# Three-neighbour interpolation on one core: fetching each batch's features 14 chunks ahead and casting them 3 chunks ahead, instead of both 6 chunks ahead

## The chip, the cores and the metric

The kernel runs on one core of one Trainium2 chip. The metric is device time in microseconds (us), lower is better. Three runs of the kernel before gave a median of 646.55 us (645.44 to 646.75).

## The reference

For each of 16 batches there are 1024 feature rows of 64 numbers, and 4096 queries. A query has three indices into the feature rows and three weights. Its result is the weighted sum of the three rows, with the weights divided by their sum:

```
weights_norm = weights / (weights_sum + 1e-8)
for b in range(batch):
    for i in range(n_query):
        for k in range(3):
            result[b, i] += weights_norm[b, i, k] * features[b, indices[b, i, k]]
```

Inputs and output are float32; the indices reach the kernel as 64-bit integers.

## The kernel before

The gather is done as a matrix product with a selection matrix that is made on the chip. The 4096 queries of a batch are cut into 8 chunks of 512, so there are 128 chunks, numbered i = 0 to 127; batch b begins at chunk a = 8b. Chunks are grouped by four (2048 queries, half a batch); only the first batch has smaller groups.

For a group, these steps follow one another:

- VectorE (DVE) prepares 16-bit codes from the indices and half-precision weights (prep, four batches at a time), and SyncE (SP) puts them into the scratch tensors code_d and wt_d.
- SP loads the codes of a group into the tile bcc (load_codes): one DMA of 1536 KB that broadcasts to all 128 partitions. It loads the weights into bcw (load_weights): two DMAs of 768 KB, one for each half of the partitions.
- ScalarE (ACT) turns codes into bytes y, one ACTIVATE for each chunk (stage1). DVE takes these apart into the four 8-bit selection matrices s (stage2).
- For each chunk, TensorE (PE) multiplies s by the batch's features f16 into the PSUM tile acc: 3 neighbours by 4 feature slices, 12 matmuls of 128x512 (main).
- acc is multiplied by the weights into x. For even chunks DVE reads acc directly; for odd chunks ACT first copies acc to xc (weight).
- Two chunks later PE sums the three neighbours and transposes with 12 small matmuls into pr. After every second chunk ACT copies pr to og, and SP writes og out (back).

The features of a batch come as one DMA of 256 KB into the tile fst (float32, two buffers), which ACT casts and halves into f16 (two buffers). In the kernel before, both are in load_features: the DMA and the cast are emitted at the same place.

The order of work on every engine is written out, and each engine works strictly in its order (InOrder, line 47). The list todo holds steps with a time in chunks. A step with time t is emitted in the iteration i that holds t: before the chunk's own work if its third entry is 0, and behind it if that entry is 1. Steps with negative times come before the chunk loop. Line 242 puts the codes at a - 12, line 243 the weights at a - 7, line 245 the features at a - 6 (a being the first chunk of the group, for line 245 of the batch), and line 247 stage1 of a group of four from a - 8 on, one chunk of it behind each iteration. For every batch but the first, the features step stands in iteration 8(b-1) + 2, the third iteration of the batch that is being worked on.

All loads and stores are issued by SP, also in order. A store of og waits on SP until ACT has written og, and whatever SP has to issue behind it waits as well. In the profile nearly every line is L55, the helper that records each operation, so operations are told apart by their tiles; f is f16, i_sb is the identity i2.

Of the kernel before, what the change touches and what calls it, by code (L numbers as in the profile page):

```python
# [9 lines left out]
P = 128  # L10
# [3 lines left out]
def kernel(  # L14
# [12 lines left out]
    fp32 = mybir.dt.float32  # L27
# [11 lines left out]
    J = 4  # L39
# [20 lines left out]
    sb = ctx.enter_context(tc.tile_pool(name="sb", bufs=2))  # L60
# [85 lines left out]
        for c in range(n // CH):  # L146
            owner[a + c] = (g, c)

    bcc, bcw, f16s, ys, ss = {}, {}, {}, {}, {}

    def load_codes(g):
        b, q, n, _ = groups[g]
# [12 lines left out]
                in_=wt_d.ap()[h, b, :, q:q + n].unsqueeze(0).to_broadcast([D, K, n]))  # L165

    def load_features(b):
        fst = sb.tile([P, J * P], fp32, bufs=2, name="fst")
        sp.dma_start(out=fst[:, :], in_=features[b].rearrange("(l x) d -> l (x d)", l=P))
        f16s[b] = sb.tile([P, J, P], fp16, bufs=2, name="f16")  # L170
        ac.mul(out=f16s[b].rearrange("p j m -> p (j m)"), in_=fst[:, :], mul=0.5)

# [64 lines left out]
    def at(time, engine, f, *args):  # L237
        todo.append((time, len(todo), engine, f, args))

    for g, (b, q, n, a) in enumerate(groups):  # L240
        m = n // CH
        at(a - 12, 0, load_codes, g)
        at(a - 7, 0, load_weights, g)
        if q == 0:
            at(a - 11.5 if b == 0 else a - 6, 0, load_features, b)
        for c in range(m):
            at(a - 2 * m + c if m == 4 else -8.5 + g / 10, 1, stage1, g, c)
        for j in range(J):
            at(a - m + (j * m // J | 1 if m == 4 else 0), 0, stage2, g, j)
# [78 lines left out]
```

## Time and profile before

| What | Value |
|---|---|
| Median of 3 runs | 646.55 us |
| Profiled execution | 649.85 us, of which its span (first to last instruction) is 647.9 us |
| Granted TensorE clock, mean | 0.837 of full speed |
| PE busy | 419.7 us, 65% of the span |
| ACT busy | 321.6 us, 50% |
| DVE busy | 306.5 us, 47% |
| DMA | 125.66 MB; the main queue's packets take 78.4% of the 16 engines' span |

Busy shares are means over the whole span. The features are cast 16 times, once a batch, so a batch's cycle can be read from one cast to the next. The chain of waits follows the work that ended last back to the start, and counts the time of each step on it. DMA share is the mean busy share of the 16 DMA engines; it can be somewhat over 1, since packets overlap.

### The profile page before, as it was taken

How to read it: one execution, taken by the hardware profiler on the slowest of the kernel's cores; microseconds unless marked ns; L12 is line 12 of the kernel's file. 1: busy time of each engine (PE TensorE's matmuls, PEld its weight loads, DVE VectorE, ACT ScalarE, POOL GpSimd, SP SyncE). 2: the span in 40 equal slices, each digit the busy share in tenths (PEclk: the TensorE clock that was granted, in tenths of full speed). 3: DMA queues.
4: the chain of work that ended last, by engine and by line, in shares of the span. 5: the costliest groups of instructions: out<-in, count | busy, mean ns of one | idle time of the engine just before them, and what ended most of it. 6: DMA issues, size and time to landing. Idle time of an engine off the chain costs nothing.

```text
span 647.9 us, 7370 instructions
## 1 busy us (share of the span) xinstructions
PE 419.7 (65%) x3072; PEld 211.8 (33%) x3072; DVE 306.5 (47%) x335; ACT 321.6 (50%) x274; POOL 0.2 (0%) x4
## 2 busy tenths in 40 slices
PE   0435492957859294793929649294875939387596
PEld 0112151523425152341514325152442515143253
DVE  4312380825537182662707338182643626164473
ACT  0531562818366370744718266371836547082642
POOL 0000000000000000000000000000000000000000
PEclk9967696997969698695968969798796959789698
DMA  5899495896959599695969959699795959669521
GB/s 89 221 207 251 134 267 113 227 251 167 267 150 283 135 240 218 151 263 132 272 138 201 278 117 279 129 230 228 188 270 137 265 133 260 166 178 267 128 62 66
DMA packets 70704, 125.66 MB, mean 194 GB/s; under 512 B 24080, under 2 KB 44048, under 8 KB 70672
## 3 DMA queue, kind: packets, MB, share of 16 engines
q1 hardware_dynamic: 70672, 125.20, 78.4%
q8 instruction: 24, 0.39, 0.3%
q14 instruction: 8, 0.07, 0.0%
HBM read 107.23 MB, written 17.96 MB: 193 GB/s over the span
## 4 chain that ended last, share of the span: by engine, by line
PE 41%; DMA 36%; ACT 10%; SPq 7%; issue 4%; DVE 2%; ACTq 0%
PE acc L55 37%; DMA fst<-in_features_dram 31%; SPq L55 7%; ACT y L55 4%; DMA bcc<-code_d 4%; PE pr L55 4%; ACT xc L55 4%; ACT og L55 1%; DVE x L55 1%; DVE s L55 1%; DMA code_d<-code 0%; DMA idx<-in_indices_dram 0%; ACTq L55 0%; ACT f L55 0%; DVE wn L55 0%
## 5 line engine op out<-in xcount | busy, mean ns | idle before, releaser
L55 PE MATMUL acc<-s,f 128*128 128x512 fp8e4 x1536 | 386.6, 406 | 222.8 <-ACT xc L55 196.7
L55 PEld LDWEIGHTS <-f 128*128 128x128 f16 x1536 | 151.0, 103 | 401.7 <-issue 244.7
L55 ACT ACTIVATE y<-bcc,lane_sb 128x1536 uint8<-128x1536 int16 x128 | 196.7, 1576 | 17.0 <-DMA bcc<-code_d 17.0
L55 DVE TENSOR_TENSOR x<-xc,bcw 128x1536 f16<-128x1536 f16 x64 | 61.3, 958 | 296.3 <-ACT xc L55 296.3
L55 ACT ACTIVATE f<-fst 128x512 f16<-128x512 f32 x16 | 10.1, 629 | 234.8 <-DMA fst<-in_features_dram 234.8
L55 ACT CAST xc<-acc 128x1536 f16<-128x1536 f32 x64 | 91.7, 1433 | 67.5 <-PE acc L55 67.5
L55 DVE TENSOR_SCALAR s<-y 128x1536 int32<-128x1536 int32 (+2 forms) x136 | 117.0, 904 | 15.4 <-ACT y L55 15.4
L55 DVE TENSOR_TENSOR x<-acc,bcw 128x1536 f16<-128x1536 f32 x64 | 112.2, 1753 | 20.8 <-PE acc L55 17.2
L55 PEld LDWEIGHTS <-x 128*128 128x128 f16 x1536 | 71.4, 117 | 30.6 <-DVE x L55 1.8
L55 PE MATMUL pr<-i_sb,x 128*128 128x64 f16 x1536 | 71.6, 197 | 1.7 <-DVE x L55 1.7
L55 ACT COPY og<-pr 128x512 f32<-128x512 f32 x64 | 37.8, 591 | 1.2 <-issue 1.2
L55 DVE RECIPROCAL wi<-ws 128x128 f32<-128x128 f32 (+2 forms) x5 | 3.9, 789 | 0.1
L55 DVE TENSOR_TENSOR wn<-wt,wi 128x128 f16<-128x128 f32 (+2 forms) x15 | 3.9, 284 | 0.1
L55 DVE COPY idk<-idx 128x384 int32<-128x384 int32 (+2 forms) x5 | 2.5, 493 | 3.0 <-DMA idx<-in_indices_dram 3.0
L55 ACT ACT_TABLE_LOAD x1 | 1.3, 1283 | 2.8 <-DMA lane_sb<-lane 2.8
L55 DVE SCALAR_TENSOR_TENSOR code<-ex,lane_i 128x384 uint16<-128x384 f32 (+2 forms) x5 | 2.4, 474 | 0.2 <-DMA code_d<-code 0.2
L55 DVE TENSOR_TENSOR wh<-wn,hb 128x384 f16<-128x384 f16 (+2 forms) x5 | 2.4, 474 | 0.1
L55 DVE TENSOR_REDUCE ws<-wt 128x128 f32<-128x384 f32 (+2 forms) x5 | 2.3, 466 | 0.0
L55 DVE TENSOR_SCALAR lane_i<-idk 128x384 int32<-128x384 int32 (+2 forms) x5 | 1.6, 315 | 0.1
L55 DVE TENSOR_SCALAR ex<-ex 128x384 int32<-128x384 int32 (+2 forms) x5 | 1.6, 315 | 0.1
L55 DVE TENSOR_TENSOR wh<-wn,wh 128x384 f16<-128x384 f16 (+2 forms) x5 | 1.6, 314 | 0.1
L55 DVE TENSOR_SCALAR ex<-idk 128x384 int32<-128x384 int32 (+2 forms) x5 | 1.6, 313 | 0.0
(8 smaller groups left out, 3.4 us busy)
## 6 DMA issues: line engine op xcount, KB each, us to landing
bcc<-code_d SPq DMA_DIRECT2D x31, 1536.0 KB, 12.0
bcw<-wt_d SPq DMA_DIRECT2D x62, 768.0 KB, 16.2
out_dram<-og SPq DMA_DIRECT2D x64, 256.0 KB, 7.4
fst<-in_features_dram SPq DMA_DIRECT2D x16, 256.0 KB, 14.6
idx<-in_indices_dram SPq DMA_DIRECT2D x3, 384.0 KB, 14.4
bcc<-code_d SPq DMA_DIRECT2D x2, 384.0 KB, 8.9
bcc<-code_d SPq DMA_DIRECT2D x1, 768.0 KB, 14.1
bcw<-wt_d SPq DMA_DIRECT2D x4, 192.0 KB, 10.8
```

Of the source, the lines that this page charges most:

```text
L55: return tc.keep_in_program_order(getattr(self.engine, op)(*a, **kw))
```

## The change

The two halves of load_features become two steps. load_features only allocates fst and issues the DMA; it keeps fst in a dictionary by batch. cast_features allocates f16 and casts. For batches 1 to 15 the fetch now stands at max(a - 14, -4), before the chunk's own work, and the cast at a - 3, behind the chunk's own work. For batch 0, the fetch stays at -11.5 and the cast stands at -8.6.

```
-    bcc, bcw, f16s, ys, ss = {}, {}, {}, {}, {}
+    bcc, bcw, fsts, f16s, ys, ss = {}, {}, {}, {}, {}, {}
...
     def load_features(b):
-        fst = sb.tile([P, J * P], fp32, bufs=2, name="fst")
+        fst = fsts[b] = sb.tile([P, J * P], fp32, bufs=2, name="fst")
         sp.dma_start(out=fst[:, :], in_=features[b].rearrange("(l x) d -> l (x d)", l=P))
+
+    def cast_features(b):
+        fst = fsts[b]
         f16s[b] = sb.tile([P, J, P], fp16, bufs=2, name="f16")
         ac.mul(out=f16s[b].rearrange("p j m -> p (j m)"), in_=fst[:, :], mul=0.5)
...
         if q == 0:
-            at(a - 11.5 if b == 0 else a - 6, 0, load_features, b)
+            at(-11.5 if b == 0 else max(a - 14, -4), 0, load_features, b)
+            at(-8.6 if b == 0 else a - 3, 1, cast_features, b)
```

On ACT, this is the stretch around the cast for batch 2 in the kernel before, whose result is called f_547. The y in front of it and the y behind it belong to two successive iterations.

```order
L55 ACTIVATE y<-bcc,lane_sb 128x1536 x2
L55 CAST xc<-acc 128x1536
L55 COPY og<-pr 128x512
L55 ACTIVATE y<-bcc,lane_sb 128x1536
L55 ACTIVATE f_547<-fst 128x512
L55 ACTIVATE y<-bcc,lane_sb 128x1536
L55 CAST xc<-acc 128x1536
L55 COPY og<-pr 128x512
```

In the changed kernel the cast for batch 2 is called f_687, and this is the stretch around it on ACT.

```order
L55 ACTIVATE y<-bcc,lane_sb 128x1536 x2
L55 CAST xc<-acc 128x1536
L55 COPY og<-pr 128x512
L55 ACTIVATE f_687<-fst 128x512
L55 ACTIVATE y<-bcc,lane_sb 128x1536 x2
L55 CAST xc<-acc 128x1536
L55 COPY og<-pr 128x512
```

The cast has moved from the iteration a - 6 to behind the work of a - 3, right after a copy to og. Nothing else changes places on ACT.

On SP, the order of the two kernels differs in two places only. The first is before the chunk loop, between codes and weights.

```order
 L55 DMA bcw<-wt_d 64x3x1024 x2
 L55 DMA bcc<-code_d 128x3x2048
+L55 DMA fst<-in_features_dram 128x512
 L55 DMA bcw<-wt_d 64x3x2048 x2
 L55 DMA bcc<-code_d 128x3x2048
```

The second is in the last batch but one.

```order
 L55 DMA bcc<-code_d 128x3x2048
 L55 DMA bcw<-wt_d 64x3x2048 x2
-L55 DMA out_dram<-og 128x2x256
-L55 DMA fst<-in_features_dram 128x512
-L55 DMA out_dram<-og 128x2x256
+L55 DMA out_dram<-og 128x2x256 x2
```

One fetch is added at the start and one is gone at the end. The 14 fetches between stand where they stood, in the third iteration of each batch, but each now brings the features of a batch one further on.

## Rows read from the trace of the kernel before

**Rows 1.** The page's chain that ended last, by engine and by line.

```profile
PE 41%; DMA 36%; ACT 10%; SPq 7%; issue 4%; DVE 2%; ACTq 0%
PE acc L55 37%; DMA fst<-in_features_dram 31%; SPq L55 7%; ACT y L55 4%; DMA bcc<-code_d 4%; PE pr L55 4%; ACT xc L55 4%; ACT og L55 1%; DVE x L55 1%; DVE s L55 1%; DMA code_d<-code 0%; DMA idx<-in_indices_dram 0%; ACTq L55 0%; ACT f L55 0%; DVE wn L55 0%
```

**Rows 2.** Who waited for whom: us in total, times, longest.

```profile
ACT f L55 <- DMA fst<-in_features_dram: 234.8, 16, 19.1
PE acc L55 <- ACT xc L55: 196.7, 16, 15.8
...
ACT y L55 <- DMA bcc<-code_d: 17.0, 4, 10.7
```

**Rows 3.** Chain in order of time, 305 to 342 us: start, us, what.

```profile
320.81 0.38 SPq L55
...
321.24 15.84 DMA fst<-in_features_dram
...
337.64 1.56 ACT y L55
339.20 1.33 ACT xc L55
```

**Rows 4.** Timeline of PE, 301.8 to 313: start, us, operation, idle before.

```profile
301.84 5.00 PE L55 MATMUL acc<-s,f 128*128 128x512 fp8e4 x12 [11.40 <-ACT xc L55]
...
307.06 2.75 PE L55 MATMUL acc<-s,f 128*128 128x512 fp8e4 x12
...
310.04 2.75 PE L55 MATMUL acc<-s,f 128*128 128x512 fp8e4 x12
```

**Rows 5.** Timeline of ACT around the casts for batches 1 and 15.

```profile
70.03 0.63 ACT L55 ACTIVATE f<-fst 128x512 f16<-128x512 f32 x1 [19.14 <-DMA fst<-in_features_dram]
...
603.34 0.63 ACT L55 ACTIVATE f<-fst 128x512 f16<-128x512 f32 x1 [14.30 <-DMA fst<-in_features_dram]
```

**Rows 6.** Windows between those casts: engines' busy us, PEclk, DMA share, GB/s.

```profile
0.00:17.00 17.00, 0.00 (x0) 0.00 (x0) 7.77 (x29) 1.74 (x3) 0.20 (x4) 1.00 0.56 95
17.00:70.03 53.03, 20.35 (x96) 8.59 (x97) 12.24 (x19) 16.89 (x12) 0.00 (x0) 0.72 0.91 215
70.03:603.34 533.31, 363.68 (x2688) 184.51 (x2688) 262.40 (x266) 279.52 (x238) 0.00 (x0) 0.84 0.82 204
603.34:647.90 44.56, 35.66 (x288) 18.75 (x287) 24.10 (x21) 23.40 (x22) 0.00 (x0) 0.88 0.31 83
```

**Rows 7.** Windows inside two batches; engine columns PE, PEld, DVE, ACT, POOL.

```profile
310.00:332.00 22.00, 18.12 (x151) 9.62 (x148) 12.24 (x11) 10.05 (x9) 0.00 (x0) 0.96 1.05 251
333.00:342.00 9.00, 1.43 (x4) 0.54 (x4) 1.45 (x2) 4.90 (x5) 0.00 (x0) 0.50 0.13 41
342.00:368.00 26.00, 24.29 (x190) 12.58 (x188) 16.27 (x15) 15.07 (x13) 0.00 (x0) 0.96 1.04 259
```

**Rows 8.** Timeline of SP (its queue), 301.8 to 328.

```profile
302.73 0.46 SPq L55 DMA_DIRECT2D bcc<-code_d  x1
...
315.22 0.54 SPq L55 DMA_DIRECT2D bcc<-code_d  x1
315.85 1.26 SPq L55 DMA_DIRECT2D bcw<-wt_d  x2
320.81 0.38 SPq L55 DMA_DIRECT2D out_dram<-og  x1
321.24 0.46 SPq L55 DMA_DIRECT2D fst<-in_features_dram  x1
```

**Rows 9.** The page's DMA issues: count, KB each, median us to landing.

```profile
bcc<-code_d SPq DMA_DIRECT2D x31, 1536.0 KB, 12.0
bcw<-wt_d SPq DMA_DIRECT2D x62, 768.0 KB, 16.2
out_dram<-og SPq DMA_DIRECT2D x64, 256.0 KB, 7.4
fst<-in_features_dram SPq DMA_DIRECT2D x16, 256.0 KB, 14.6
```

**Rows 10.** Timeline of ACT, 314.5 to 322.

```profile
314.64 3.05 ACT L55 ACTIVATE y<-bcc,lane_sb 128x1536 uint8<-128x1536 int16 x2
```

**Rows 11.** Codes tile bcc alone: landing times over all its loads.

```profile
DMA to landing us min/median/max: 6.5/12.0/21.2
```

## The prediction

> **What bounds the kernel now.** I read the chain that ended last first. A transfer of 256 KB a batch, the features, holds 31% of it, almost as much as the matmuls into acc [rows 1]. The list of waits says who stands still for it: ACT, 16 times, 234.8 us in all, and through ACT's copy to xc also PE, 16 times, 196.7 us [rows 2]. The other transfer that ACT reads, the codes, cost it only 17.0 us [rows 2].
>
> The chain in order of time shows how one stall comes about. SP issues the fetch at 321.24, it lands 15.84 us later, and only after the cast can ACT do the y and the xc on which PE waits [rows 3]. On PE the stall is 11.40 us of idle time, and the 12 matmuls behind it take 5.00 us instead of 2.75 [rows 4]; the granted clock is then at the lower level, 0.50 of full speed, as the stalled window shows [rows 7]. Between stalls PE starts a chunk every 310.04 - 307.06 = 2.98 us [rows 4], so 8 chunks need 23.84 us.
>
> From the cast for batch 1 at 70.03 to that for batch 15 at 603.34 [rows 5] there are 14 batches in 533.31 us, 38.09 each, so 14.25 us of each batch is stall and restart. In this stretch PE is busy 363.68/14 = 26.0 us a batch, ACT 20.0, DVE 18.7, and the DMA engines 0.82 of 38.09 = 31.2 us, moving 204 GB/s x 38.09 us = 7.77 MB [rows 6]. The DMA engines thus have more work per batch than any compute engine. Their load is uneven: 1.05 and 1.04 at 251 and 259 GB/s while PE computes, 0.13 at 41 GB/s in the end of a stall [rows 7]. The reason is on SP: behind the fetch stands a store of og that waits for ACT, so for as long as ACT waits nothing more is issued. The fetch is the last entry before the stall, and the DMA queue runs empty [rows 8].
>
> **The change, part by part.** *The cast moves to a - 3.* Its fetch was issued 11 chunks earlier, at least 11 x 2.98 = 32.8 us, against a landing time of 14.6 us [rows 9] and 15.84 in the stall shown. The wait should be gone in all 15 batches that have it; the one for batch 0 stays. The cast's own 0.63 us [rows 5] remains: ACT has 20.0 us of work a batch, so it hides. Both buffers of fst and f16 are free in time: the tile that batch b overwrites belonged to batch b - 2, whose cast lies 5 chunks before the fetch and whose last matmul lies 6 chunks before the cast.
>
> *The fetch moves one batch forward.* SP has one more entry at the start and one fewer at the end; in between the list is the same, so no transfer is pushed behind another. The added one costs 256 KB at 251 GB/s, 1.0 us, in the start.
>
> *What is late next.* PE alone would let a batch run in 23.84 us, ACT and DVE in less. The DMA engines would not: with 31.2 us of work and a filled share of 1.04 they need 30.0 us; by bytes, 7.77 MB at 251 to 259 GB/s, 30.0 to 31.0 us. So DMA takes the bound over. I take 30.5, hence a gain of 38.09 - 30.5 = 7.6 us a batch, and 14 x 7.6 = 106 us. Only half of the stall comes back.
>
> *Does the DMA queue stay filled?* The next wait should be ACT's for codes. Codes are issued for instance at 302.73 and 315.22 [rows 8], some 12.5 us apart, and read by the second y of the pair that starts at 314.64 [rows 10], at about 316.2: 13.4 us after the issue, against 12.0 us median landing [rows 9]. When ACT waits there, SP has already issued behind those codes the weights of a group (two of 768 KB), two stores, and the next codes. That is some 3.6 MB, about 14 us of transfers at 251 GB/s, where behind the features there was nothing. So ACT's short waits should not drain it. They may cost PE the lower clock, 5.00 - 2.75 = 2.25 us each; two a batch give 23.84 + 4.5 = 28.3 us, still below 30.5, so this is hidden. The unknown is how well it stays filled. Bounds from rows: 30.0 us a batch at best; at worst the share of the start-up stretch, 0.91 [rows 6], where transfers and engines wait for each other: 31.2/0.91 = 34.3 us, a gain of 3.8 a batch, 53 us. I stay near the good end, because the saturated windows of 22 and 26 us were reached with the same order on SP.
>
> *Start and end.* From 17.0 to 70.03 us the DMA engines do 53.03 x 0.91 = 48.3 us of work [rows 6], which at 1.04 would take 46.4: up to 6.6 us to gain, and 19.14 us of ACT's wait lies there [rows 5]. I take 6; bounds: -1 (the added 256 KB) and 12. After 603.34 the DMA share is 0.31 [rows 6], so this end is PE's in both kernels. What goes there is the refill behind the cast (0.54 + 1.56 + 1.33 us [rows 3, 5]) and the half-clock chunk, about 5 us; a last wait for codes may take some back. I take 4; bounds 0 and 8.
>
> **The sum.** Span 647.9 - 106 - 6 - 4 = 532 us. The profiled execution took 649.85 us, 1.95 more than its span, so 534; it was 0.5% above the median of the runs shown, 646.55, so 3 us come off: 531 us. With the bounds: 14 x 8.1 + 12 + 8 = 133 gives 514; 53 - 1 + 0 = 52 gives 594.
>
> Where the TensorE clock is concerned, no more than that enters the sum. On transfers, the Trainium skill, DMA: Bandwidth & Descriptors, section "Where 436 GB/s comes from", says that between HBM and SBUF a core's HBM limit of about 358 GB/s binds. By that, 7.77 MB would take an estimated 21.7 us a batch, less than PE's 23.84, and DMA would not be the bound. The trace disagrees: at a share of 1.04 to 1.05 it moves 251 to 259 GB/s [rows 7].
>
> **The rivals.**
>
> *A, DMA gives way and PE becomes the bound.* If the busy share overstates the engines' load (a packet's time holds waiting too), deeper queueing could raise the rate over 300 GB/s. Then a batch takes 23.84 us, the gain is 14 x 14.25 = 200, and with start and end the time is 437 us. Against it: the rate stays within 251 to 259 GB/s in both long filled stretches. Chance 4%. The skill's rule above would lead here, too.
>
> *B, the wait moves to the codes or the weights and the queue drains again, only less.* ACT and SP are both in order, and a store behind ACT can still block SP. With the start-up share of 0.91 the time is 594 us; for 0.94 to 0.91, some 575 to 594. For it: codes have only about 1.4 us to spare at full pace. Against: the 3.6 MB behind them. Chance 14%.
>
> *C, slower: each wait for codes is longer than the features' wait it replaces.* Place: the second y of each group, twice a batch. If landing rises to the longest seen, 21.2 us [rows 11], each wait is 21.2 - 13.4 = 7.8 us plus the restart of 2.25: 23.84 + 2 x 10.05 = 43.9 us a batch, 5.8 more than now, about 728 us. It decides from 23.84 + 2(W + 2.25) = 38.09, W = 4.9 us, a landing time of 18.3 us. Against: such landings mean a full queue, and a queue that is always full finishes a batch in about 30 us; C needs long landings and an idle queue together. Chance 4%.
>
> *D, nothing is won:* the change doesn't do what it says, because SP reaches the earlier fetch so late that the cast still waits, or the DMA stretches by as much as the stall shrinks. The time stays 646 us. For the first, the fetch would have to land 33 us after its turn; the longest wait before was 19.1 us [rows 2]. Chance 2%.
>
> **How the numbers follow.** The forecast (DMA-bound, 531 us) has 76%; its own range is 514 to 560, the latter with a share of 0.96 (31.2/0.96 = 32.5 us a batch). With B the range of 8 in 10 is 508 to 592: it leaves out A, C, D and the edges of the forecast and of B. About 0.2% is what a measurement of this kernel can tell from no change. Faster by more: forecast, A and B, 94%; within 0.2%: 2% (D); slower: 4% (C).
>
> **What the profile after would show.** Right: ACT's wait for fst is one of some 12 us (batch 0) instead of 234.8 in 16; the chain's 31% for the features is gone and codes or weights stand in their place; from cast to cast 30 to 31 us; the DMA share in that stretch is 1.0 or more at about 250 GB/s; the 0.50 clock is rarer. ACT's waits for codes rise over 17 us, to some 5 us a batch. Wrong: a DMA share still near 0.85 in the middle (B), a rate over 300 GB/s with PE's row nearly full (A), waits for codes over 4.9 us twice a batch (C), or casts that still wait (D).

## The result and the profile after

The changed kernel takes 527.33 us (median of 4 runs, 525.81 to 529.4) against 646.0 us for the kernel before: a ratio of 0.817, 95% interval 0.813 to 0.821. The forecast was 531. The profiled execution took 525.81 us, its span is 523.7. Ratios and intervals, here and below, leave out executions that took over 1.5% more than the fastest of their kernel; the medians have all of them.

The page's chain that ended last, by engine and by line, answers to [rows 1].

```profile
DMA 61%; ACT 12%; PE 10%; SPq 6%; issue 6%; DVE 4%; ACTq 0%
DMA bcc<-code_d 55%; PE acc L55 10%; SPq L55 6%; ACT xc L55 6%; ACT y L55 4%; DMA out_dram<-og 4%; DVE x L55 2%; ACT og L55 2%; DMA fst<-in_features_dram 2%; DVE s L55 1%; ACT f L55 1%; PE pr L55 1%; DMA idx<-in_indices_dram 0%; DMA code_d<-code 0%; ACTq L55 0%
```

The features fell from 31% to 2%, and the codes rose from 4% to 55%. The list of waits (us in total, times, longest) says the same of ACT, beside [rows 2].

```profile
ACT y L55 <- DMA bcc<-code_d: 148.5, 33, 10.6
...
PE acc L55 <- ACT xc L55: 68.2, 29, 11.6
...
ACT f L55 <- DMA fst<-in_features_dram: 12.8, 1, 12.8
```

Fifteen of the sixteen waits for features are gone. ACT now waits 33 times for codes, two times a batch, and PE's wait behind ACT is a third of what it was. The timeline of ACT has the casts for batches 1, 2 and 15; none has idle time in front of it.

```profile
62.80 0.64 ACT L55 ACTIVATE f<-fst 128x512 f16<-128x512 f32 x1
95.78 0.64 ACT L55 ACTIVATE f<-fst 128x512 f16<-128x512 f32 x1
...
489.81 0.64 ACT L55 ACTIVATE f<-fst 128x512 f16<-128x512 f32 x1
```

The windows between them (columns as in [rows 6]) give the sum.

```profile
0.00:62.80 62.80, 23.93 (x122) 10.47 (x123) 22.00 (x51) 26.78 (x22) 0.20 (x4) 0.89 0.83 196
62.80:489.81 427.01, 361.90 (x2714) 184.40 (x2713) 263.66 (x269) 278.41 (x240) 0.00 (x0) 0.96 1.01 259
489.81:523.70 33.89, 27.96 (x240) 14.97 (x237) 19.31 (x17) 15.15 (x16) 0.00 (x0) 0.95 0.23 79
```

Fourteen batches take 427.01 us, 30.50 each, against 38.09 [rows 6]: 106.3 us less. In this stretch the DMA share is 1.01 instead of 0.82; the work in it, 30.8 us a batch, is nearly the old one (31.2). What lies before the first and behind the last of these casts shrank from 70.03 + 44.56 = 114.6 to 96.7 us, 17.9 less. (The casts now stand three chunks later, at both ends of the stretch, so only the two pieces together can be compared.) 106.3 + 17.9 = 124.2 us is the difference of the spans, 647.9 - 523.7.

How a wait for codes looks is seen in the chain in order of time, 250 to 283 us.

```profile
260.08 13.75 DMA bcc<-code_d
...
273.93 0.04 ACT y L55
...
275.42 1.42 ACT xc L55
```

On the queue of SP in the changed kernel, from those codes on:

```profile
260.08 0.46 SPq L55 DMA_DIRECT2D bcc<-code_d  x1
260.63 1.67 SPq L55 DMA_DIRECT2D bcw<-wt_d  x2
262.62 0.64 SPq L55 DMA_DIRECT2D out_dram<-og  x1
264.49 0.36 SPq L55 DMA_DIRECT2D fst<-in_features_dram  x1
269.05 0.37 SPq L55 DMA_DIRECT2D out_dram<-og  x1
269.46 0.47 SPq L55 DMA_DIRECT2D bcc<-code_d  x1
270.03 5.87 SPq L55 DMA_DIRECT2D bcw<-wt_d  x2
```

When the codes issued at 260.08 land at 273.83, more weights, two stores, the features and the next codes have already been issued. Behind the features in [rows 8] nothing was: the next entry on SP in the kernel before is a store 19.8 us after that fetch.

```profile
341.04 0.37 SPq L55 DMA_DIRECT2D out_dram<-og  x1
```

So in the changed kernel the queue has no time to run empty. That the DMA engines then set the pace is what the experiments test.

### The profile page after: what moved, and what is told of

Read it like the earlier page. It is cut to its first block, busy times and chain, and to the rows that moved or that the text cites. A ratio compares the mean times of both kernels' runs of the same rounds, so it can differ in the third digit from the quotient of the medians.

```text
span 523.7 us, 7372 instructions
## 1 busy us (share of the span) xinstructions
PE 413.8 (79%) x3072; PEld 209.8 (40%) x3072; DVE 305.0 (58%) x335; ACT 320.3 (61%) x274; POOL 0.2 (0%) x4
## 4 chain that ended last, share of the span: by engine, by line
DMA 61%; ACT 12%; PE 10%; SPq 6%; issue 6%; DVE 4%; ACTq 0%
DMA bcc<-code_d 55%; PE acc L55 10%; SPq L55 6%; ACT xc L55 6%; ACT y L55 4%; DMA out_dram<-og 4%; DVE x L55 2%; ACT og L55 2%; DMA fst<-in_features_dram 2%; DVE s L55 1%; ACT f L55 1%; PE pr L55 1%; DMA idx<-in_indices_dram 0%; DMA code_d<-code 0%; ACTq L55 0%
## 5 line engine op out<-in xcount | busy, mean ns | idle before, releaser
L55 PE MATMUL acc<-s,f 128*128 128x512 fp8e4 x1536 | 377.7, 394 | 104.5 <-ACT xc L55 68.2
L55 ACT ACTIVATE y<-bcc,lane_sb 128x1536 uint8<-128x1536 int16 x128 | 198.3, 1577 | 148.5 <-DMA bcc<-code_d 148.5
L55 PEld LDWEIGHTS <-f 128*128 128x128 f16 x1536 | 148.4, 101 | 278.9 <-issue 119.0
L55 DVE TENSOR_SCALAR s<-y 128x1536 int32<-128x1536 int32 (+2 forms) x136 | 117.1, 905 | 14.6 <-ACT y L55 14.5
L55 ACT CAST xc<-acc 128x1536 f16<-128x1536 f32 x64 | 91.4, 1428 | 30.8 <-PE acc L55 30.8
L55 PEld LDWEIGHTS <-x 128*128 128x128 f16 x1536 | 71.9, 117 | 31.2 <-DVE x L55 1.8
L55 ACT ACTIVATE f<-fst 128x512 f16<-128x512 f32 x16 | 10.2, 640 | 12.8 <-DMA fst<-in_features_dram 12.8
## 6 DMA issues: line engine op xcount, KB each, us to landing
bcc<-code_d SPq DMA_DIRECT2D x31, 1536.0 KB, 18.9
bcw<-wt_d SPq DMA_DIRECT2D x62, 768.0 KB, 20.1
```

Of the source, the lines that this page charges most:

```text
L55: return tc.keep_in_program_order(getattr(self.engine, op)(*a, **kw))
```

## The experiments

Theory T: the DMA engines set the pace as soon as nothing empties their queue, and in the kernel before SP, held by the store behind the fetch, let it run empty in every batch. The ratios below are to the kernel before, with 95% intervals; the changed kernel has 0.817 (0.813 to 0.821).

**Only the fetch early.** The cast goes back to 6 chunks ahead.

```
-            at(-8.6 if b == 0 else a - 3, 1, cast_features, b)
+            at(-8.6 if b == 0 else a - 6, 0, cast_features, b)
```

> The fetch stands 14 chunks ahead as in the changed kernel, the cast 6 chunks ahead as before. Theory T (the 16 DMA engines set the pace at 30.5 us a batch as soon as nothing empties their queue): a cast that doesn't wait costs its 0.64 us wherever it stands, so 527 us within 5. Rival R1 (the later place of the cast on ACT brings part of the gain, by keeping it out of the way of the copy to xc): 540 to 580 us.

Measured: 526.62 us, ratio 0.815 (0.811 to 0.819), as the changed kernel. R1 is out: the cast's later place adds nothing.

**Only the cast late.** The fetch goes back to 6 chunks ahead.

```
-            at(-11.5 if b == 0 else max(a - 14, -4), 0, load_features, b)
+            at(-11.5 if b == 0 else a - 6, 0, load_features, b)
```

> The fetch stands 6 chunks ahead as before, the cast 3 chunks ahead as in the changed kernel. Landing takes about 16 us and the cast comes some 11 us after the fetch was issued, so ACT still waits about 5 us a batch for the features. Theory T: by then SP has issued a store, codes and weights behind the fetch, the queue stays filled, and the wait takes the place of one for codes: 527 to 540 us. Rival R2 (the length of ACT's wait is what counts, not the queue): 15 waits of 5 us more, some 600 us.

Measured: 537.66 us, ratio 0.829 (0.821 to 0.836). Its list of waits:

```profile
ACT y L55 <- DMA bcc<-code_d: 89.4, 29, 11.0
ACT f L55 <- DMA fst<-in_features_dram: 88.1, 16, 12.5
```

ACT waits 88.1 us for the features, but its wait for codes is 59 us shorter than in the changed kernel, and the window between the casts for batches 1 and 15 shows the pace unchanged: 428.99/14 = 30.64 us a batch, share 1.01.

```profile
68.27:497.26 428.99, 360.11 (x2688) 184.46 (x2688) 258.66 (x262) 279.11 (x238) 0.00 (x0) 0.96 1.01 257
```

R2 is out. PE's pace of 23.84 us and the wait left in front of these casts (69.1/14 = 4.9 us a batch) come to 28.8 us, less than the DMA engines' work, so this wait costs nothing of its own. Either half of the change alone brings nearly all of it, since SP has then issued something else between the fetch and the wait for it. Why this run is about 1% slower than the changed kernel (0.829 against 0.817) was not settled.

**Stores from GpSimd, in the kernel before.** Fetch and cast stay together in the program, 6 chunks ahead; only SP is no longer held by stores.

```
-    pe, ve, ac, sp = (InOrder(e) for e in (nc.tensor, nc.vector, nc.scalar, nc.sync))
+    pe, ve, ac, sp, po = (InOrder(e) for e in (nc.tensor, nc.vector, nc.scalar, nc.sync, nc.gpsimd))
...
-            sp.dma_start(
+            po.dma_start(
                 out=out[b, (c - 1) * CH:(c + 1) * CH].rearrange("(c i u) d -> i c (u d)", c=2, u=U),
```

> The kernel before, fetch and cast both 6 chunks ahead, but the stores of og are issued by GpSimd, so that SP is not held by the store behind the fetch and goes on to the next codes while ACT waits. Theory T (half of the stall was an empty queue, because SP was held): the codes, 1.5 MB, fill 4 to 6 us of the 8 empty ones, then SP is held by the weights' buffer: 560 to 600 us, with ACT still waiting over 10 us a batch for the features. Rival R2 (ACT's wait itself is the cost): 646 us.

Measured: 545.21 us, ratio 0.842 (0.837 to 0.846), less than expected (560 to 600). Rows of its waits, of SP's queue, of ACT and of the window between the casts for batches 1 and 15:

```profile
ACT f L55 <- DMA fst<-in_features_dram: 128.2, 16, 18.4
PE acc L55 <- ACT xc L55: 90.5, 16, 15.2
```

```profile
298.99 0.60 SPq L55 DMA_DIRECT2D fst<-in_features_dram  x1
299.69 0.39 SPq L55 DMA_DIRECT2D bcc<-code_d  x1
```

```profile
17.08 0.63 ACT L55 ACTIVATE f<-fst 128x512 f16<-128x512 f32 x1 [12.69 <-DMA fst<-in_features_dram]
70.56 0.63 ACT L55 ACTIVATE f<-fst 128x512 f16<-128x512 f32 x1 [18.42 <-DMA fst<-in_features_dram]
...
313.09 0.63 ACT L55 ACTIVATE f<-fst 128x512 f16<-128x512 f32 x1 [9.34 <-DMA fst<-in_features_dram]
```

```profile
70.56:497.46 426.90, 363.37 (x2688) 184.97 (x2688) 262.48 (x266) 279.52 (x238) 40.82 (x56) 0.91 0.92 254
```

Codes now follow the fetch at once, and the DMA share between the casts rises from 0.82 to 0.92. SP also runs ahead: this fetch is issued at 298.99, 4.8 us before ACT begins to wait for it (313.09 - 9.34 = 303.75); in the kernel before it was 1.0 us (321.24, and 337.10 - 14.84 = 322.26). Both shorten ACT's wait. In front of the casts for batches 2 to 15 it is 128.2 - 12.69 - 18.42 = 97.1 us, 6.9 a batch, against 203.2 us, 14.5 a batch, summed in the same way over ACT's timeline in the kernel before.

A batch takes 426.90/14 = 30.49 us. That this is the changed kernel's number is a coincidence: the share of 0.92 leaves 2.4 us a batch without transfers, so the DMA engines are not the bound here. PE's pace of 23.84 us and the wait of 6.9 come to 30.7, and in the kernel before 23.84 + 14.5 = 38.3 against 38.09 measured. In both kernels, then, ACT's wait is paid in full. R2's time of 646 us is out, because the wait shrank, but what R2 says of its price holds for these two kernels; the cast-late run above shows where it ends. The 20.1 us by which the span of this run (543.8) is longer than the changed kernel's lie in start and end: 116.9 us against 96.7.

**Stores from GpSimd, in the changed kernel.** The same edit, to see what it does by itself.

> The changed kernel with the stores of og issued by GpSimd instead of SP. With the kernel before, this move left a queue that moved 276 to 280 GB/s when filled, against 264 to 267 in the changed kernel. Theory T, with a pace that depends on what stands side by side in the queues: the engines' work falls as there, by some 25 us, and the time is 500 us (490 to 512). Rival R8 (a filled queue is worth the same however it is filled): 527 us within 6.

Measured: 512.65 us, ratio 0.796 (0.791 to 0.801), just above T's range (490 to 512) and 13 us above its 500. The window between the casts for batches 1 and 15 gives 411.66/14 = 29.40 us a batch.

```profile
62.30:473.96 411.66, 360.94 (x2714) 184.19 (x2713) 263.71 (x269) 277.92 (x240) 41.08 (x56) 0.96 1.02 270
```

So a separate queue for stores is worth 1.1 us a batch in the changed kernel, where SP is not held behind the fetch. Of the 7.6 us that it brought in the kernel before, some 6.5 would be left for the end of SP's hold, if the two effects simply add; no run shows that they do.

**Four more loads behind the fetch,** 1.05 MB a batch into unused buffers, in the changed kernel and in the kernel before.

```
         sp.dma_start(out=fst[:, :], in_=features[b].rearrange("(l x) d -> l (x d)", l=P))
+        for _ in range(4 if b else 0):
+            ex = sb.tile([P, J * P], fp32, bufs=4, name="extra")
+            sp.dma_start(out=ex[:, :], in_=features[b].rearrange("(l x) d -> l (x d)", l=P))
```

> The changed kernel with four more loads of 256 KB into unused buffers, issued right behind the fetch of the features of each batch but the first: 1.05 MB more a batch. Theory T (the DMA engines set the pace): at 259 GB/s each batch is 4.05 us longer, 15 x 4.05 = 61 us, so 588 us (575 to 600). Rival R4 (the lead of the codes paces it, the engines have room): under 540 us.

> The kernel before with the same four loads, behind its fetch. Theory T: behind the fetch the queue runs empty, and the 9 us with a DMA share of 0.13 have room for these 4 us of transfers: 646 us within 6. Rival R5 (the kernel before was paced by the DMA engines' work too): 61 us more, some 707 us.

Measured: 573.4 us in the changed kernel (0.882, 0.875 to 0.889), 46 us more; 648.86 us in the kernel before (1.001, 0.998 to 1.004), nothing. The kernel before with these loads, two windows of one batch, the first in the end of the stall, the second while PE computes:

```profile
326.00:335.30 9.30, 1.57 (x18) 0.91 (x17) 0.00 (x0) 0.00 (x0) 0.00 (x0) 0.69 0.99 269
307.00:326.00 19.00, 19.00 (x151) 10.02 (x150) 13.35 (x12) 12.49 (x11) 0.00 (x0) 1.00 1.06 269
```

The hole of [rows 7], with its share of 0.13, is filled to 0.99, and the time does not move. R5 is out. In the changed kernel there is no hole, and every batch pays 46/15 = 3.1 us. T had asked for 4.05, so the time is just below its range (575 to 600); counted this way the added loads moved at 1.05 MB/3.1 us = 340 GB/s, faster than the mean of the queue.

**Codes 16 chunks ahead,** with a fourth buffer, in the changed kernel.

```
-        bcc[g] = sb.tile([P, K * GM], i16, bufs=3, name="bcc")[:, 0:K * n]
+        bcc[g] = sb.tile([P, K * GM], i16, bufs=4, name="bcc")[:, 0:K * n]
...
-        at(a - 12, 0, load_codes, g)
+        at(a - 16 if a >= 16 else a - 12, 0, load_codes, g)
```

> The changed kernel with the codes issued 16 chunks ahead instead of 12 and a fourth buffer for them. Theory T: ACT's waits for codes are the engines' pace, an earlier issue lets the queue grow longer but not faster; the wait moves to the weights or stays: 527 us within 10. Rival R4 (the lead of the codes paces the changed kernel): the 148.5 us of waits for codes vanish and the time goes to 440 to 490 us.

Its runs took 550.17, 559.38, 563.9 and 1067.56 us, so far apart that no ratio is given; even the fastest is 4% above the slowest run of the changed kernel (529.4). R4 is out, but T, which asked for the same time within 10 us, missed it too. Its list of waits and the window between the casts for batches 1 and 15:

```profile
ACT og L55 <- DMA out_dram<-og: 133.1, 26, 8.3
DVE x L55 <- DMA bcw<-wt_d: 72.4, 20, 6.9
```

```profile
65.35:514.23 448.88, 371.06 (x2714) 186.85 (x2713) 267.39 (x270) 277.78 (x240) 0.00 (x0) 0.94 1.00 244
```

ACT waits for codes only 21.7 us in all instead of 148.5; it waits for stores to land, so that og is free, and DVE waits for weights. The share is 1.00 as before, the rate 244 GB/s instead of 259. Why the same bytes in another order move more slowly was not settled.

**Weights loaded for six groups only,** in the changed kernel.

```
+        if g >= 6:
+            bcw[g] = bcw[5]
+            return
```

> As the changed kernel, but weights are loaded for the first six groups only, and every later group uses the weights of the sixth: 40% of the bytes are gone, with all computation left in (the output is then not the reference's). Theory T: the DMA engines have some 16 to 18 us of work a batch, PE takes the bound at 23.84 us: 527 - 14 x 6.7 = 433 us, up to 450. Rival R4 (what paces the changed kernel is the lead of the codes, issued 12 chunks ahead but read from 4 or 5 chunks after their issue, and not the engines' work): ACT's waits for codes stay, 500 us or more.

Measured: 440.42 us, ratio 0.682 (0.678 to 0.685), in T's range. The window between the casts for batches 1 and 15:

```profile
62.99:404.18 341.19, 339.09 (x2696) 179.02 (x2695) 266.22 (x269) 279.54 (x239) 0.00 (x0) 0.99 0.69 197
```

A batch takes 341.19/14 = 24.4 us, PE is busy in 339.09 of the 341.19 us, and the DMA share is 0.69. With the DMA bound gone, PE's pace of 23.84 us a batch [rows 4] is nearly all that remains.

**Half of the weights from GpSimd's queue,** in the changed kernel.

```
...
-            sp.dma_start(
+            (po if h else sp).dma_start(
                 out=bcw[g][h * D:(h + 1) * D],
```

> As the changed kernel, but the second half of each weights load (partitions 64 to 127) is issued by GpSimd instead of SP, so the two halves stand in different queues. Theory T says only that the bytes and the engines' work set the pace: if the engines' work for these bytes is the same, 527 us within 8. Rival R3 (a load to one half of the partitions runs at about 205 GB/s where a load to all runs at about 400, and two halves of different queues overlap): 3.7 us less for each of two groups, 23 us of DMA work a batch, PE takes the bound, 440 to 470 us.

Measured: 515.94 us, ratio 0.795 (0.788 to 0.802): 11 us less than the changed kernel, just outside T's band and far from R3's. Issuing the halves from two queues is not enough, though in most groups the two are issued within 1.4 us of each other (for instance at 266.57 and 266.79). Whether they overlapped on the DMA engines, no run here shows.

**The weights as one load to 128 partitions,** in the changed kernel.

```
-        for h in range(2):
-            sp.dma_start(
-                out=bcw[g][h * D:(h + 1) * D],
-                in_=wt_d.ap()[h, b, :, q:q + n].unsqueeze(0).to_broadcast([D, K, n]))
+        sp.dma_start(
+            out=bcw[g], in_=wt_d.ap()[0, b, :, q:q + n].unsqueeze(0).to_broadcast([P, K, n]))
```

> The changed kernel, but the weights of a group come as one load to 128 partitions instead of two loads to 64 each: the same bytes, but both halves then hold the first half's weights, so the output is not the reference's. Rival R3 (a load to one half of the partitions is slow in itself): weights go from about 205 GB/s to nearer 400, DMA work falls by up to 7 us a batch, PE takes the bound: 440 to 470 us. If the bytes alone count: 527 us within 8.

Measured: 431.12 us, ratio 0.665 (0.661 to 0.669). The window between the casts for batches 1 and 15:

```profile
60.62:395.13 334.51, 334.51 (x2690) 177.55 (x2688) 262.80 (x265) 279.83 (x240) 0.00 (x0) 1.00 0.97 325
```

As many bytes a batch move at 325 instead of 259 GB/s, and PE is busy without a gap; the time is even below R3's range (440 to 470). This run also reads only one half's rows from memory; the next pair of runs does without that.

**The two halves interleaved over all partitions,** in the changed kernel and in the kernel before. This keeps the two loads and the whole computation.

```
-    i2_np = np.concatenate([np.eye(D), np.eye(D)], 0).astype(np.float16)
+    i2_np = np.repeat(np.eye(D), 2, 0).astype(np.float16)
...
-                out=bcw[g][h * D:(h + 1) * D],
+                out=bcw[g][h:P:2],
...
-        ac.mul(out=f16s[b].rearrange("p j m -> p (j m)"), in_=fst[:, :], mul=0.5)
+        ac.mul(out=f16s[b].rearrange("p j (d h) -> p j h d", h=2),
+               in_=fst.rearrange("p (j h d) -> p j h d", h=2, d=D), mul=0.5)
```

> The changed kernel with feature dimension d and half h in partition 2d + h instead of 64h + d (the cast writes f16 in that order, the identity i2 follows), so each of the two weights loads of a group goes to every second partition over all 128. The same bytes, two loads as before. If a load is slow because it goes to one half of the partitions only, DMA work falls as with one load to 128 partitions and PE takes the bound at 23.9 us a batch: 430 to 450 us. Rival R6 (a load to 64 partitions is slow wherever they lie, or two loads cost more than one): 500 to 530 us.

> The kernel before (fetch and cast both 6 chunks ahead) with the same interleaved halves. Theory T: the stall of a batch is the queue's backlog in front of the fetch plus about 8 us in which the queue is empty; the backlog shrinks by the 7 us saved on weights, the empty time stays, so about 31 us a batch: 545 us (515 to 570), some 100 us slower than the changed kernel with interleaved halves. Rival R7 (with less DMA work the fetch lands in time and its place no longer matters): under 470 us.

Measured: 434.91 us on the changed kernel (0.672, 0.670 to 0.674), 562.64 us on the kernel before (0.870, 0.866 to 0.875). The first is faster than both kernels of this case. R6 and R7 are out. The window between the casts for batches 1 and 15, in the changed kernel with interleaved halves:

```profile
59.22:397.77 338.55, 336.18 (x2696) 178.17 (x2694) 262.82 (x265) 280.92 (x239) 0.00 (x0) 1.00 0.97 323
```

And in the kernel before with interleaved halves:

```profile
58.02:512.88 454.86, 365.48 (x2688) 185.63 (x2688) 262.50 (x266) 280.99 (x239) 0.00 (x0) 0.89 0.77 239
```

Of two loads with the same bytes, those that go to every second partition move like one load to all. With them a batch takes 24.2 us where the features come early, and 32.5 where the fetch stands at its old place with the queue running empty: a share of 0.77 of 32.5 us leaves 7.5 us without transfers. In the kernel before, 0.82 of 38.09 leaves 6.9 us [rows 6]. Here too ACT's wait is paid in full: in front of the casts for batches 2 to 15 it comes to 121.6 us, 8.7 a batch, and with PE's 23.84 that is 32.5.

## Why the prediction was right

*The wait for features would go in 15 batches of 16, and hide at 11 chunks of lead.* Right: 12.8 us in one wait are left.

*DMA takes the bound at 30.5 us a batch, so half of the stall comes back.* Right: 30.50. That it is met to the digit is luck, since the rows gave 30.0 to 31.0. That the changed kernel is bound by DMA is shown from both sides: more bytes cost time in the changed kernel and none in the kernel before, fewer bytes or faster ones give PE's pace of about 24 us.

*The DMA engines' load is uneven because SP is held behind the fetch and the queue runs empty.* Right: SP's next entry comes 19.8 us later, four more loads put into the hole cost nothing, and with the stores on another queue the codes follow the fetch at once and the DMA share rises to 0.92. But the empty queue is not what the wait costs. In the kernel before, and with the stores on GpSimd, a batch is PE's pace plus ACT's wait; the wait costs nothing only where the DMA engines' work is longer than this sum, as in the cast-late run. The forecast went by the same two terms: 14.25 us of stall, of which the DMA engines' work leaves only about half to gain.

*Start and end give 6 + 4 = 10 us (bounds -1 to 20).* Too low: 17.9, and the start is the term that was mis-sized. In the kernel before, the matmuls of chunks 5 and 117 stand right behind the casts at 70.03 and 603.34 [rows 5]. In the changed kernel the same matmuls start without idle time at these places:

```profile
56.41 2.75 PE L55 MATMUL acc<-s,f 128*128 128x512 fp8e4 x12
...
482.37 2.75 PE L55 MATMUL acc<-s,f 128*128 128x512 fp8e4 x12
```

Counted to these, the start gives 70.03 - 56.41 = 13.6 us, above its bound of 12, and the end 44.56 - 41.33 = 3.2. The bound had taken all 48.3 us of transfers up to the cast at 70.03 for work that must be done first. The changed kernel reaches the place with 39.41 x 0.97 = 38.2 us of them:

```profile
17.00:56.41 39.41, 20.45 (x97) 8.65 (x98) 13.20 (x20) 21.70 (x16) 0.00 (x0) 0.83 0.97 235
```

*The sum, 532 us against a span of 523.7, and 531 us against 527.33.* The sum is off by 8 us, all of it in start and end; that the forecast is off by only 4 is luck. It took 3 us off because the profiled execution of the kernel before was slower than the median; that of the changed kernel was 1.5 us faster than its median.

*ACT's waits for codes rise to some 5 us a batch.* Too low: 148.5/16 = 9.3 us. The pace is as forecast, so more of the wait than thought lies in ACT's spare time (30.5 less 20.0 us of work).

*Rival C would decide from a landing time of 18.3 us for codes.* That point was wrong as a sign. The median landing is now 18.9 us, 12.0 before [rows 9], and C's slower time is not seen:

```profile
bcc<-code_d SPq DMA_DIRECT2D x31, 1536.0 KB, 18.9
```

Loads take longer to land with the queue filled, and a batch at 30.5 us gives each load more time than one at full pace. C's own sum, with the 4.6 us that a wait for codes takes on average between the two casts, would be 23.84 + 2 x (4.6 + 2.25) = 37.5 us a batch, against 30.50. It priced each of ACT's waits in full on PE, but PE stood behind ACT for only 68.2 us in all, ACT behind the codes for 148.5.

*The rate of the filled queue, 251 to 259 GB/s, as a limit of the DMA engines.* Good for this change (259), but not a limit of the engines: it is a mean over loads of different rates. A load to one half of the partitions has a low one. Two windows of 1 us in the changed kernel show it; by the order on SP and the landing at 273.83, the first falls on the codes issued at 260.08, the second on the weights behind them:

```profile
269.00:270.00 1.00, 1.00 (x8) 0.42 (x5) 1.00 (x1) 1.00 (x2) 0.00 (x0) 1.00 1.03 426
274.00:275.00 1.00, 1.00 (x15) 0.68 (x14) 0.00 (x0) 1.00 (x1) 0.00 (x0) 1.00 1.04 205
```

Codes to all partitions move at 426 GB/s, weights to one half at 205, both at a full share. And 323 GB/s came with the same bytes laid out otherwise. The Trainium skill, DMA: Bandwidth & Descriptors, section "The descriptor swizzle", has partitions 0 to 63 behind one set of eight SBUF ports and 64 to 127 behind another; the runs agree so far as loads that touch both have the higher rate, though no run here shows a port.

The Trainium skill's 358 GB/s, weighed ahead of the result (DMA: Bandwidth & Descriptors, section "Where 436 GB/s comes from"), is not borne out as a limit: the window above has 426. But the forecast's reason against it, a filled queue at 251 to 259 GB/s, came from the half-partition loads. With these gone, what it led to did come true: PE was the bound, at 323 and 325 GB/s.

## What to carry to other kernels

When an engine waits for a DMA, look at what the issuing queue has behind that DMA. If an entry there waits for the engine that waits, no transfers are issued for as long as it waits, and any one break of the circle helps: here an earlier fetch, a later use and another queue for the entry behind it each took a batch from 38.09 to some 30.5 us. Price what a removed wait can win by the next resource's work in the same stretch, not by the length of the wait: a batch took the longer of two times, PE's pace plus the wait left, and the DMA engines' work. When the DMA engines then set the pace, compare the GB/s of the single loads: partitions that a load covers can matter more than its bytes.

## What the runs showed that I had not expected

Two loads of 768 KB to partitions 0 to 63 and 64 to 127, against the same bytes to 128 partitions or to every second one: 259 GB/s against 325 and 323 over 14 batches, and 30.8 us of DMA work a batch against 24.2 x 0.97 = 23.5. Issuing the two from different queues brought only 11 us of the 92 that interleaving brought. And a longer lead for the codes made the kernel slower, at the same DMA share and a lower rate (244 GB/s); its cause stays open.
